# Rotary embedding over split heads: eight tiles of 8 rows a partition in place of a mix of 4 and 8, with the rows dealt anew to VectorE and TensorE

## The chip, the core and the metric

The kernel runs on one core of one Trainium2 chip. A core has five engines that run side by side: TensorE (PE, with its weight loads shown as PEld), VectorE (DVE), ScalarE (ACT), GpSimd (POOL) and SyncE (SP). Data moves between the device's memory (HBM) and the on-chip SBUF over 16 DMA engines. A DMA is issued from a queue; here ScalarE issues the loads and SyncE the stores. PSUM is the small memory that TensorE writes and that VectorE and ScalarE read. The metric is the device time of one execution in microseconds (us), as a median over runs; a change of under 0.5% is taken as no change.

## The reference

```
x = x.reshape(16, 512, 16, 64)                 # batch, seq, heads, head_dim
x1, x2 = x[..., :32], x[..., 32:]
cos = cos[None, :, None, :]                    # seq x 32
sin = sin[None, :, None, :]
rotated = concatenate([x1 * cos - x2 * sin, x1 * sin + x2 * cos], axis=-1)
```

x has 16 x 512 rows of 1024 float32 (4 KB), 33.55 MB in all, and the result has the same size. Each element of the result is the sum of two products: the element times a cosine, and its partner in the other half of the head times a sine with a sign. cos and sin depend on the place in the sequence alone and are 64 KB each.

## The kernel before

A "row" below is one row of x in each of 128 partitions, 128 x 1024 elements (512 KB). There are 64 of them, numbered u = 0 to 63. A batch of 512 rows gives each partition 4 consecutive rows (R1 = 4, a "single", 16 KB a partition); a pair of batches gives each partition 8 (R2 = 8, 32 KB a partition). Batches 0, 1, 14 and 15 are singles, the other twelve are six pairs, so there are ten tiles of 4, 4, 8, 8, 8, 8, 8, 8, 4 and 4 rows. They live in a ring of 40 rows in SBUF (x_sb) and are worked on in place.

Each row takes three steps. First, t1 = x times cosine, on VectorE, from SBUF into one of three PSUM slots (line 293). Second, t2 = x with its halves swapped, times the signed sine, into one of six SBUF slots; GpSimd does this (line 257) except for row 3 of each pair, which VectorE does (line 286, the list V2). Third, the sum t1 + t2 goes back over x. For most rows VectorE adds (line 304, called comb below). For the rows of the list PE2 (rows 1, 3 and 6 of each eight, outside the first and last four rows, 21 in all) TensorE adds t2 to t1 in PSUM by multiplying with the identity (line 224) and ScalarE copies PSUM to SBUF (line 191).

VectorE's order is written out by hand: for u = 0, 1, 2 ... it issues the cosine product of row u (with the sine product ahead of it, if row u is in V2) and then the sum of row u - 1, if that is VectorE's. The cosine product of row u must wait until the PSUM slot of row u - 3 is free, which for a row of PE2 is ScalarE's copy.

The sine and cosine tables are needed in two layouts. For singles VectorE copies the cosine (line 264) and ScalarE the sine (lines 182 and 183) straight from the staged tables. For pairs TensorE picks the staged rows into PSUM (line 208) and ScalarE copies the sine out with both signs (lines 186 and 187).

ScalarE issues six loads (40 rows) and the two tables at the start (lines 153 and 174). The other loads go over places of the ring whose rows must first be stored. ScalarE issues them in the midst of its copies, after the row with LAG = 10 added to the last row that held the place, that is after u = 17, 25 and 33, and waits there for the store of that place (line 146). SyncE issues one store a tile (line 161), when the tile's last row is added.

```
    singles = (0, 1, batch - 2, batch - 1)
    tiles = [(b, R1 if b in singles else R2) for b in range(batch) if b in singles or b % 2 == 0]
    V_ROW = 3
    PE2 = [R1 <= u < NU - R1 and u % R2 in (1, 3, 6) for u in range(NU)]
    V2 = [tiles[t][1] == R2 and r == V_ROW for t, r in rows]
```

Of the kernel before, what the change touches and what calls it, by code (L numbers as in the profile page):

```python
# [6 lines left out]
def bass_split_heads_rope_kernel(  # L7
# [9 lines left out]

    batch, seq, dim = x.shape
# [5 lines left out]
    R2 = 2 * R1  # L30
    assert R1 * P == seq and R1 == 4 and batch % 2 == 0
# [8 lines left out]
    singles = (0, 1, batch - 2, batch - 1)  # L40
    tiles = [(b, R1 if b in singles else R2) for b in range(batch) if b in singles or b % 2 == 0]
    NT = len(tiles)
    RING = 5 * R2

    rows = [(t, r) for t, (_, n) in enumerate(tiles) for r in range(n)]
    NU = len(rows)
    EARLY = (NU - RING) // R2


    V_ROW = 3  # L50
    PE2 = [R1 <= u < NU - R1 and u % R2 in (1, 3, 6) for u in range(NU)]
    V2 = [tiles[t][1] == R2 and r == V_ROW for t, r in rows]

# [12 lines left out]
    LAG = 10  # L66

    with ExitStack() as stack:
# [3 lines left out]
        s1_sb = stack.enter_context(nc.sbuf_tensor([P, R1, 2, HALF], fp32))  # L72
        s2_sb = stack.enter_context(nc.sbuf_tensor([P, R2, 2, HALF], fp32))
        ident = stack.enter_context(nc.sbuf_tensor([P, P], fp32))
        pick = stack.enter_context(nc.sbuf_tensor([P, 2, 2, P // 2], fp32))
        zero = stack.enter_context(nc.sbuf_tensor([P, BANK], bf16))
        tab_ps = stack.enter_context(nc.psum_tensor([P, BANK], fp32))
        pair_ps = stack.enter_context(nc.psum_tensor([P, 2, 2, R1, HALF], fp32))
        t1_ps = stack.enter_context(nc.psum_tensor([P, NT1, H * HD], fp32))
        sem_in = [stack.enter_context(nc.semaphore(f"in{t}")) for t in range(NT)]  # L80
        sem_out = [stack.enter_context(nc.semaphore(f"out{k}")) for k in range(EARLY)]
# [3 lines left out]
        sem_c = stack.enter_context(nc.semaphore("ctab"))  # L85
        sem_s = stack.enter_context(nc.semaphore("stab"))
        sem_z = stack.enter_context(nc.semaphore("zero"))
# [7 lines left out]
        sem_t = stack.enter_context(nc.semaphore("pairs"))  # L95
        sem_a = stack.enter_context(nc.semaphore("act"))

        c1_ps = tab_ps[:, 0:R1 * HALF].rearrange("p (r d) -> p r d", d=HALF)
        v_ps = tab_ps[:, R1 * HALF:R1 * HALF + HD].rearrange("p (t d) -> p t d", d=HALF)

        def c_of(t, r):
            return c1_ps[:, r, :] if tiles[t][1] == R1 else pair_ps[:, r // R1, 0, r % R1, :]

        def s_of(t, r):
            return s1_sb[:, r] if tiles[t][1] == R1 else s2_sb[:, r]

        x1 = x.rearrange("b (s r) d -> b s (r d)", r=R1)
        o1 = out.rearrange("b (s r) h d -> b s (r h d)", r=R1)
        x2 = x.rearrange("b s d -> (b s) d").rearrange("(g p r) d -> g p (r d)", p=P, r=R2)
        o2 = out.rearrange("b s h d -> (b s) h d").rearrange("(g p r) h d -> g p (r h d)", p=P, r=R2)  # L110
        xs = x_sb[:].rearrange("p n h t d -> p n (h t d)")

        def in_dram(single, pairs, t):
            b, n = tiles[t]
            return single[b] if n == R1 else pairs[b // 2]

        def in_sbuf(t):
            b, n = tiles[t]
            k = b * R1 % RING
            return x_sb[:, k:k + n].rearrange("p n h t d -> p (n h t d)")  # L120

        def where(u):
            t, r = rows[u]
            return t, r, u % RING

# [6 lines left out]
        def wait_added(eng, u):  # L132

            if n_pe[u]:
                eng.wait_ge(sem_a, n_pe[u])
            if n_comb[u]:
                eng.wait_ge(sem_v, n_comb[u])

        def wait_t2_free(eng, u):

# [7 lines left out]
        def stores_of(k):  # L148

            return sum(b * R1 // R2 == k for b, _ in tiles)  # L150

        def load(eng, t):
            eng.dma_start(in_sbuf(t), in_dram(x1, x2, t)).then_inc(sem_in[t], 16)  # L153

        def on_sync(sp):
            for u in range(NU):
                t, r, k = where(u)
                if r == tiles[t][1] - 1:
                    wait_added(sp, u)
                    k = u // R2  # L160
                    sp.dma_start(in_dram(o1, o2, t), in_sbuf(t)).then_inc(sem_out[k] if k < EARLY else sem_rest, 16)
            sp.wait_ge(sem_rest, 16 * sum(stores_of(k) for k in range(EARLY, NU // R2)))

        def on_scalar(ae):
            later = {}
            for t, (b, n) in enumerate(tiles):
                if b * R1 + n <= RING:
                    load(ae, t)
                else:

                    later.setdefault((b * R1 - RING) // R2 * R2 + R2 - 1 + LAG, []).append(t)
                if t == 0:
                    for i, (table, sem) in enumerate(((cos, sem_cos), (sin, sem_sin))):
                        ae.dma_start(stage[:, i, :], table.rearrange("(s r) d -> s (r d)", r=R1)).then_inc(sem, 16)  # L174

            ae.wait_ge(sem_i, 2)
            ae.activation(  # L177
                pick[:], ident[:].rearrange("q (s k) -> q k s", k=2)[:, :, None, :].broadcast_to([P, 2, 2, P // 2]), COPY
            ).then_inc(sem_g, 1)
# [54 lines left out]
        def on_gpsimd(pl):  # L234
# [11 lines left out]
            for u in range(NU):  # L246
                if V2[u]:
                    continue
                t, r, k = where(u)
                if (t, r) == (0, 0):  # L250
                    pl.wait_ge(sem_s, 1)
# [103 lines left out]
```

## Time and profile before

| what | value |
|---|---|
| median of 3 runs (161.09 to 161.94) | 161.11 us |
| the profiled execution's own time (its span, first to last instruction) | 160.0 us |
| median less that span | 1.1 us |
| bytes moved in the span, mean rate | 67.26 MB, 420 GB/s |
| busy: VectorE, GpSimd, TensorE, ScalarE | 130.1, 134.9, 73.7, 24.4 us |
| mean granted TensorE clock | 0.710 of full speed |
| DMAs on ScalarE's queue / SyncE's queue | 12 (33.69 MB) / 10 (33.56 MB) |

The page gives busy time for each engine as a share of the span, and the DMA line gives the mean share of the core's 16 DMA engines that were busy in each of 40 slices. The profile gives no time of that execution other than the span. Lines such as "ACT x_sb L191 <- PE t_ps L224: 98.9" say that ScalarE, at line 191, sat idle for 98.9 us in all until TensorE's line 224 was done. A DMA's "us to landing" runs from its issue to the arrival of its last byte, so it includes the time that it stands in its queue.

### The profile page before, as it was taken

To read this page: it belongs to the slowest core of one execution; us is meant where nothing else is said; L and a number is where in the kernel's file an instruction comes from. 1 tells how busy PE (TensorE), PEld (TensorE's weight loads), DVE (VectorE), ACT (ScalarE), POOL (GpSimd) and SP (SyncE) were. 2 spreads that over 40 slices of the span, in tenths; PEclk is the share of its full clock that TensorE was granted. 3 is DMA by queue.
4 is the path that set the end of the run, shared out by engine and by line. 5 is a ranking of instruction groups with operands and counts; after the bars stand their busy time and mean duration, and the time that the engine had idled before them with its cause. 6 is when DMAs were issued, how large, how long until landed. Compare 5 with 4: busy or idle time off the path is not lost.

```text
span 160.0 us, 522 instructions
## 1 busy us (share of the span) xinstructions
PE 73.7 (46%) x94; PEld 23.7 (15%) x94; DVE 130.1 (81%) x117; ACT 24.4 (15%) x27; POOL 134.9 (84%) x64
## 2 busy tenths in 40 slices
PE   6050005476427735690948606459439841970000
PEld 1020002021102220220222002002202210320000
DVE  0069998699999998997989709899999989989600
ACT  0420000205020502022022020220220122050000
POOL 1059999999999999999999999698999999289400
PEclk9999999969955865567555685855855599577555
DMA  5999999999999999999999999999999999999997
GB/s 160 401 451 463 401 430 418 410 483 406 401 463 406 494 401 401 483 426 401 467 426 418 410 467 434 401 467 393 420 463 446 418 414 418 479 410 434 414 414 303
DMA packets 3170, 67.26 MB, mean 420 GB/s; under 512 B 352, under 2 KB 608, under 8 KB 608
## 3 DMA queue, kind: packets, MB, share of 16 engines
q10 hardware_dynamic: 1728, 33.69, 49.7%
q1 hardware_dynamic: 1440, 33.56, 48.8%
q14 instruction: 2, 0.02, 0.0%
HBM read 33.69 MB, written 33.55 MB: 420 GB/s over the span
## 4 chain that ended last, share of the span: by engine, by line
DMA 59%; POOL 22%; PE 5%; DVE 3%; issue 2%; ACTq 1%; ACT 1%; DVEq 0%
DMA x_sb<-in_x_dram 41%; POOL t_sb L257 22%; DMA out_dram<-x_sb 18%; PE t_ps L224 5%; DVE x_sb L304 2%; DVE t_ps L293 1%; ACT x_sb L191 1%; ACTq L153 1%; ACTq L174 1%; DVEq L303 0%
## 5 line engine op out<-in xcount | busy, mean ns | idle before, releaser
L257 POOL TENSOR_TENSOR t_sb<-x_sb,s_sb 128x1024 f32<-128x1024 f32 x58 | 134.2, 2358 | 14.2 <-ACT s_sb L183 8.2
L224 PE MATMUL t_ps<-t_sb,ident 128*128 128x512 f32 x84 | 68.9, 973 | 62.8 <-DVE t_ps L293 37.9
L293 DVE TENSOR_TENSOR t_ps<-x_sb,pair_ps 128x1024 f32<-128x1024 f32 x48 | 57.7, 1223 | 9.7 <-ACT x_sb L191 9.7
L304 DVE TENSOR_TENSOR x_sb<-t_ps,t_sb 128x1024 f32<-128x1024 f32 x43 | 52.4, 1218 | 2.1 <-POOL t_sb L257 2.1
L191 ACT ACTIVATE x_sb<-t_ps 128x1024 f32<-128x1024 f32 x21 | 21.5, 1024 | 110.6 <-PE t_ps L224 98.9
L224 PEld LDWEIGHTS t_ps<-t_sb,ident 128*128 128x128 f32 x84 | 21.8, 286 | 109.6 <-DVE t_ps L293 70.0
L293 DVE TENSOR_TENSOR t_ps<-x_sb,tab_ps 128x1024 f32<-128x1024 f32 x16 | 19.3, 1222 | 0.5 <-ACT x_sb L191 0.5
L286 DVE TENSOR_TENSOR t_sb<-x_sb,tab_ps 128x1024 f32<-128x1024 f32 x6 | 7.3, 1212 | 0.0
L264 DVE COPY tab_ps<-stage 128x128 f32<-128x128 f32 x1 | 0.3, 295 | 7.7 <-DMA stage<-in_cos_dram 7.7
L208 PE MATMUL pair_ps<-stage,pick 128*128 128x256 f32 x4 | 2.0, 667 | 5.1 <-DMA stage<-in_sin_dram 5.1
L201 PE MATMUL t_ps<-zero 128*128 128x512 bf16 x6 | 2.7, 630 | 1.3 <-DVE zero L262 1.3
L208 PEld LDWEIGHTS pair_ps<-stage,pick 128*128 128x128 f32 x4 | 1.2, 324 | 6.2 <-issue 6.0
L177 ACT ACT_TABLE_LOAD x1 | 1.3, 1283 | 5.0 <-issue 5.0
L201 PEld LDWEIGHTS t_ps<-zero 128*128 128x128 bf16 x6 | 0.7, 138 | 2.3 <-DVE zero L262 1.2
L262 DVE MEMSET zero<- 128x256 uint32 x1 | 0.3, 272 | 0.9 <-PEq L337 0.9
L182 ACT ACTIVATE s_sb<-stage 128x128 f32<-128x128 f32 x1 | 0.3, 310 | 2.3 <-DMA stage<-in_sin_dram 2.3
L186 ACT ACTIVATE s_sb<-pair_ps 128x256 f32<-128x256 f32 x1 | 0.4, 384 | 1.7 <-PE pair_ps L208 1.7
L235 POOL MEMSET ident<- 128x128 f32 x1 | 0.2, 205 | 0.3 <-POOLq L337 0.3
L177 ACT ACTIVATE pick<-ident 128x256 f32<-128x256 f32 x1 | 0.4, 430 | 0.0
L187 ACT ACTIVATE s_sb<-pair_ps 128x256 f32<-128x256 f32 x1 | 0.4, 377 | 0.0
L237 POOL TENSOR_SCALAR_AFFINE_SELECT ident<-ident 128x128 f32<-128x128 f32 x1 | 0.3, 294 | 0.1
L337 POOL MEMSET const-float32-0.0<- 128x1 f32 x1 | 0.1, 99 | 0.3 <-issue 0.3
(6 smaller groups left out, 1.0 us busy)
## 6 DMA issues: line engine op xcount, KB each, us to landing
x_sb<-in_x_dram ACTq DMA_DIRECT2D x6, 4096.0 KB, 38.1
out_dram<-x_sb SPq DMA_DIRECT2D x6, 4096.0 KB, 25.3
x_sb<-in_x_dram ACTq DMA_DIRECT2D x4, 2048.0 KB, 22.4
out_dram<-x_sb SPq DMA_DIRECT2D x4, 2048.0 KB, 14.9
stage<-in_cos_dram ACTq DMA_DIRECT2D x1, 64.0 KB, 7.6
stage<-in_sin_dram ACTq DMA_DIRECT2D x1, 64.0 KB, 7.3
```

The lines of the kernel that those rows point to most:

```text
L153: eng.dma_start(in_sbuf(t), in_dram(x1, x2, t)).then_inc(sem_in[t], 16)
L174: ae.dma_start(stage[:, i, :], table.rearrange("(s r) d -> s (r d)", r=R1)).then_inc(sem, 16)
L177: ae.activation(pick[:], ident[:].rearrange("q (s k) -> q k s", k=2)[:, :, None, :].broadcast_to([P, 2, 2, P // 2]), COPY).then_inc(sem_g, 1)
L186: ae.activation(s2[:, :, :, 0, :], pair_ps[:, :, 1, :, :], COPY, scale=-1.0)
L191: ae.activation(xs[:, u % RING, :], t1_ps[:, u % NT1, :], COPY).then_inc(sem_a, 1)
L201: pe.matmul(t1_ps[:, k, b * BANK:(b + 1) * BANK], zero[:, 0:P], zero[:], start=True, stop=True).then_inc(sem_w, 1)
L208: pe.matmul(pair_ps[:, k].rearrange("p c r d -> p (c r d)"), pick[:, k].rearrange("q b s -> q (b s)"), stage[:].rearrange("q c f -> q (c f)"),
L224: ins = pe.matmul(t1_ps[:, u % NT1, b * BANK:(b + 1) * BANK], ident[:], t2[:, b * BANK:(b + 1) * BANK], start=False, stop=True, skip_group ...
L257: pl.tensor_tensor(t2_sb[:, u % NT2, :, :, :], swapped(k), over_heads(s_of(t, r)), mult).then_inc(sem_p, 1)
L286: ve.tensor_tensor(t2_sb[:, u % NT2, :, :, :], swapped(k), over_heads(v_ps), mult)
L293: ve.tensor_tensor(t1_ps[:, u % NT1, :].rearrange("p (h d) -> p h d", d=HALF), x_sb[:, k, :, :, :].rearrange("p h t d -> p (h t) d"), c_of ...
L304: ve.tensor_tensor(xs[:, k, :], t1_ps[:, u % NT1, :], t2_sb[:, u % NT2, :, :, :].rearrange("p h t d -> p (h t d)"), add,).then_inc(sem_v, 1)
```

## The change

Every tile has 8 rows (32 KB a partition), so one layout of the tables is left. Tile k takes rows 8k to 8k + 7, still in a ring of 40 rows. Only the load of tile 0 and the store of tile 7 are cut into two DMAs of 4 rows. There are 9 loads, 9 stores and the 2 tables: 20 DMAs in place of 22. The early loads (rows 0 to 39) have the same order and the same sizes as before. The late loads (tiles 5, 6 and 7) are issued behind rows 17, 25 and 33, as before, and wait for the stores of tiles 0, 1 and 2; the last is now one DMA of 8 rows, not two of 4.

The rows are dealt anew. PE2 is every odd row from 3 to 59 (29 rows, 21 before). V2 is rows 3 and 6 of each tile (16 rows, 6 before). GpSimd keeps 48 rows (58 before), and VectorE adds 35 rows (43 before). The rows of the first tile, whose first four took their tables straight from the staged ones, now wait for TensorE's picking too: TensorE picks cosine and sine in four matmuls of 128 columns (two of 256 before), the sine through one of the t1 slots. VectorE makes its own signed sines (two small instructions) ahead of row 2.

```diff
-    singles = (0, 1, batch - 2, batch - 1)
-    tiles = [(b, R1 if b in singles else R2) for b in range(batch) if b in singles or b % 2 == 0]
-    NT = len(tiles)
-    RING = 5 * R2
...
-    V_ROW = 3
-    PE2 = [R1 <= u < NU - R1 and u % R2 in (1, 3, 6) for u in range(NU)]
-    V2 = [tiles[t][1] == R2 and r == V_ROW for t, r in rows]
+    TILES = (
+        (8, 0, (4, 4), (8,), ()),
+        (8, 8, (8,), (8,), ()),
+        (8, 16, (8,), (8,), ()),
+        (8, 24, (8,), (8,), ()),
+        (8, 32, (8,), (8,), ()),
+        (8, 0, (8,), (8,), (0,)),
+        (8, 8, (8,), (8,), (1,)),
+        (8, 16, (8,), (4, 4), (2,)),
+    )
+    RING = 40
+
+    BEHIND = {6: 17, 7: 25, 8: 33}
...
+    V_ROWS = {8: (3, 6)}
+    V2 = [r in V_ROWS[TILES[t][0]] for t, r in rows]
+
+    PE2 = [2 <= u < NU - R1 and u % 2 == 1 for u in range(NU)]
...
         def on_scalar(ae):
...
+            early = [i for i in range(len(loads)) if i not in late]
+            for i in early:
+                load(ae, i)
...
-            ae.wait_ge(sem_sin, 16)
-            sv = stage[:, 1, :].rearrange("s (r d) -> s r d", d=HALF)
-            ae.activation(s1_sb[:, :, 0, :], sv, COPY, scale=-1.0)
-            ae.activation(s1_sb[:, :, 1, :], sv, COPY).then_inc(sem_s, 1)
...
+            for i, n in enumerate(SIZES):
+                ae.wait_ge(sem_t, i + 1)
+                ae.activation(s_sb[n][:, :, 0, :], raw_sin[n], COPY, scale=-1.0)
+                ae.activation(s_sb[n][:, :, 1, :], raw_sin[n], COPY).then_inc(sem_s, 1)
             for u in range(NU):
                 if PE2[u]:
                     ae.wait_ge(sem_e, n_pe[u])
...
+                for i in late:
+                    if BEHIND[i] == u:
+                        for j in TILES[loads[i][0]][4]:
+                            ae.wait_ge(sem_out[j], 16)
+                        load(ae, i)
...
+            for n in SIZES:
+                for c, to in enumerate((c_ps[n], raw_sin[n])):
+                    for k in range(n // R1):
+                        ins = pe.matmul(
+                            to[:, k * R1:(k + 1) * R1, :].rearrange("p r d -> p (r d)"),
+                            pick[n][:, k].rearrange("q b s -> q (b s)"),
+                            stage[:, c, :],
+                            start=c == 0,
+                            stop=True,
+                            skip_group_check=c == 1,
+                        )
+                ins.then_inc(sem_t, 1)
...
+            def own_sines():
+                ve.wait_ge(sem_s, len(SIZES))
+                for n in SIZES:
+                    v = V_ROWS[n]
+                    some = raw_sin[n][:, v[0]:v[-1] + 1:max(1, v[-1] - v[0]), :]
+                    ve.tensor_scalar_mul(v_ps[n][:, :, 0, :], some, -1.0).then_inc(sem_k, 1)
+                    ve.tensor_copy(v_ps[n][:, :, 1, :], some).then_inc(sem_k, 1)
+                ve.wait_ge(sem_k, 2 * len(SIZES))
...
+                if u == NT1 - 1:
+                    own_sines()
```

## The prediction

> **What bounds the kernel now.** I read the page first, its slices and its DMA queues, then three long windows, then the DMA issues one by one, and last the waits and the stretch around the longest one. The page's slices show how full the DMA engines are:
>
> ```profile
> DMA  5999999999999999999999999999999999999997
> GB/s 160 401 451 463 401 430 418 410 483 406 401 463 406 494 401 401 483 426 401 467 426 418 410 467 434 401 467 393 420 463 446 418 414 418 479 410 434 414 414 303
> q10 hardware_dynamic: 1728, 33.69, 49.7%
> q1 hardware_dynamic: 1440, 33.56, 48.8%
> ```
>
> The two queues' packets fill 98.5% of 16 engines' span: only 2.4 of 160.0 us are not DMA. The view by windows (columns: time, busy PE, PEld, DVE, ACT, POOL, then clock, DMA share, GB/s) splits this into loads alone, both queues, and stores alone:
>
> ```profile
> 2.50:20.00 17.50, 3.54 (x8) 1.48 (x6) 10.58 (x10) 2.88 (x6) 10.38 (x5) 1.00 0.98 416
> 24.00:138.00 114.00, 64.00 (x78) 20.26 (x79) 103.34 (x93) 19.46 (x19) 110.51 (x48) 0.67 1.00 431
> 140.50:158.00 17.50, 2.44 (x4) 0.67 (x2) 9.42 (x9) 1.59 (x2) 9.24 (x4) 0.60 0.98 422
> ```
>
> Whichever queue has work, the engines are full and the rate stays near 430 GB/s. So the DMA engines bound the kernel, one queue is enough to fill them, and the compute engines matter only where they leave both queues empty. The end shows how near that is, in the timeline (start, duration) and the DMA issues in the window of the last store:
>
> ```profile
> 149.84 1.23 DVE L304 TENSOR_TENSOR x_sb<-t_ps,t_sb 128x1024 f32<-128x1024 f32 x1 [0.67 <-POOL t_sb L257]
> 151.14 0.33 SPq L161 DMA_DIRECT2D out_dram<-x_sb  x1
> ...
> out_dram<-x_sb SPq DMA_DIRECT2D x1, 2048.0 KB, 8.8
> ```
>
> The last store is issued at 151.1 and lands at 160.0. In the packet records a 16 KB packet takes 0.611 us and a 32 KB one 1.213; the store has 8 of 16 KB on each engine, 4.9 us. So it stood about 3.6 us behind the store before it: compute has a few us to spare. Around the longest wait ScalarE and VectorE show this:
>
> ```profile
> ACT x_sb L191 <- DMA out_dram<-x_sb: 3.6, 1, 3.6
> 92.80 2.31 ACTq L153 DMA_DIRECT2D x_sb<-in_x_dram  x2
> 95.16 1.02 ACT L191 ACTIVATE x_sb<-t_ps 128x1024 f32<-128x1024 f32 x1 [8.17 <-issue]
> 96.21 1.23 DVE L293 TENSOR_TENSOR t_ps<-x_sb,pair_ps 128x1024 f32<-128x1024 f32 x1 [5.09 <-ACT x_sb L191]
> 97.50 3.78 PE L224 MATMUL t_ps<-t_sb,ident 128*128 128x512 f32 x4 [7.05 <-DVE t_ps L293]
> ```
>
> ScalarE waits for a store before it may issue a late load; its next copy is late, and VectorE loses 5.1 us. This wait stays in the change.
>
> **The change, part by part.** *DMA bill.* 256 pairs of 16 KB packets become single 32 KB ones: 256 x (2 x 0.611 - 1.213) = 2.3 us over 16 engines, 0.15 us less. Two DMAs fewer: nothing, since no window shows a gap at their joints. The early loads are the same. A DMA bound gives 160.0 - 0.15 = 159.85 us, if a queue is always filled. The rest is that question.
>
> *Tables.* They start when the staged tables are in, at 9.1. Before, four passes of 256 columns took 2.05 us; now eight of 128, each with its weight load (0.32). Least: the same 2.05. Most: nothing overlaps, 8 x (0.32 + 0.26) = 4.6. I take 2.9, eight weight loads with the passes under them, because line 224's loads (0.34) do lie under its passes. ScalarE's two copies took 0.7 (11.23 to 11.89). GpSimd starts at 12.8, not 9.6. Covered by 20 MB of loads already queued (49 us).
>
> *Tile 0.* GpSimd's pitch is 2.315 (20.82 / 9), so row 0's sine product ends at 15.15 and VectorE's first sum at 16.3. Its small sine instructions (0.19 each and a wait, 0.4 in all) and eleven more operations at its back-to-back pitch of 1.133 (120.87 to 125.40 in four) end row 7's product at 29.2. TensorE adds 3.78 at half clock (1.98 at full, as at 36.62) and ScalarE 1.02: the first store goes at 34.1, or 32.3 at full clock; before it was 20.25. That costs nothing while loads fill the engines.
>
> *Balance.* GpSimd goes from 58 to 48 rows, 111 us. VectorE goes from 64 + 6 + 43 = 113 to 64 + 16 + 35 = 115 operations, 130 us, and is now the slowest. A tile is 14 of them, 15.9 us. TensorE's four rows at half clock take 15.1 us, so they fit. From the end of a cosine product to ScalarE's release is 3.78 + 1.02 + 0.13 = 4.93 us against four VectorE operations between (4.5); that wait comes once a tile (behind V2 rows there are five operations) at 0.49, as a release at 102.37 shows. A tile is 16.35 us. GpSimd needs 13.9 and runs ahead in the six slots.
>
> *Stores and loads.* With both queues on 32 KB packets each gets half: 19.4 us per 4 MB, as in the stores that landed at 73.2 and 92.8 (issue plus time to landing). The first store before had its first packet 3.6 us after issue, behind loads. So stores 0, 1, 2 land at 34.1 + 3.6 + 19.4 + 0.6 = 57.7, then 77.2 and 96.7. Loads run alone until 37.7 (9.7 us a tile), then at half rate: tiles 3 to 7 land at 48, 68, 87, 107 and 126. Before, the last load came at 140.4. From 126 the store queue has three tiles left: it is the one to be kept full.
>
> *ScalarE's waits.* Tile 2 starts on VectorE at 46.7; behind row 17 (copied at 54.4) the wait until 57.7 holds up nothing, since ScalarE's next copy is due at 57.9. Behind row 25 (70.7) the wait lasts until 77.2 and VectorE loses 2.6 us. Behind row 33 it waits for store 2, at 96.7: with issue (0.33) and copy (1.02) VectorE goes on at 98.2 from row 38 and has lost 3 us more. Compute after that hangs on store 2. SyncE and TensorE wait behind it in their own order only; GpSimd has filled its slots.
>
> *The tail.* From 98.2 VectorE has 3 + 14 + 14 + 16 = 47 operations (the last tile has two more sums, having no TensorE rows after 59): 53.3 us, three waits of 0.49, and the last sum's end: 153.0. At full clock store 2 is 1.8 earlier and the waits go: 149.8. Needed: the bound's end 159.85 less 0.35 (last packet to end) less 4.9 puts the last store's first packet at 154.6; a queue that isn't shared starts 1.0 after issue (first load: 0.81 to 1.83), so the issue is due by 153.6. It makes it, by 0.6 at half clock and 3.8 at full. Tile 6's last copy (138.2, due by 139.1) and the first half of tile 7 (146.6, due by 148.8) also do. So the sum is 159.85, and with the 1.1 by which the median stands over this profile's span, 161.0: no change.
>
> [...]
>
> **The rivals.** *The last store comes too late (slower).* The mechanism is ScalarE's wait for store 2, from which all of the last 47 VectorE operations hang. It decides from 153.6, one us for each. For it: the slack is 0.6 at half clock; tables at 4.6 cost 1.7 of it; an issue like the second half of the 2.31 above (1.94, not 0.33) costs 1.6; a queue latency of 3.6 costs 2.6. Against: before, full clock came back in stretch after stretch, and a store behind another is already in the queue while that runs. Two of these at half clock, say the tables and the issue, put it at 156.3, so 2.7 late: 163.7. One: 162.1. As its time I take 162.8.
>
> *The last load is late as before (slower).* If it landed at 140.4 as before, a whole tile would follow: 16 x 1.133 + 0.5 = 18.6, then 1.0 + 4.9 + 0.35: 165.3, median 166.4. Against: the late half tiles then had 16 KB packets against 32 KB stores, a third of the rate; now halves meet.
>
> *DMAs cost something apiece (faster).* The packet records hold 1.4 us of longer packets, 0.86 at the start and 0.54 mostly near 22 to 27 where the first store joined. If the joining falls away and the rows' ends are more even over the engines (first engine lands at 158.9, last at 160.0), the gain is some 1.1: 160.0. Against: the start is unchanged and the joining only moves.
> [...]
>
> **How the numbers follow.** 0.5% of 161.1 is 0.8 us, about what a measurement of this kernel tells from no change. No change 0.67, at 161.0; the late last store 0.23; the late load 0.03; faster 0.07. The last three lie beyond 0.8 us. The range goes from 160.2 (most of the faster case) to 163.3 (most of the late store, up to about two of its costs).
>
> **What would show it.** Right: DMA share still about 98% with both queues together; first store near 32 to 34; last load landing near 126; VectorE waiting for ScalarE near 75 and 95; last store issued between 150 and 153.6; its time to landing over 6. Wrong: a DMA gap in the last slices and a last store that lands within some 6 us of issue; loads landing after 130; windows with both queues above 435 GB/s.

## The result

The change made the kernel a little slower. Its median is 162.11 us (161.9 to 162.78, six runs) against 161.38 us (161.09 to 161.94, six runs) for the kernel before on the same chip: a ratio of 1.0053, with an interval of 1.0034 to 1.0072. (Ratios and their 95% intervals, here and below, compare the fast runs alone and are not the quotients of the medians beside them.) A second set on another chip gave 161.86 against 161.34, 1.0028 [1.0009, 1.0047]. So the loss is 0.3 to 0.5%, where 161.0 and "no change" were forecast; the time lies inside the forecast range of 160.2 to 163.3. Against the 0.5% set ahead as the line for no change, the first set lies just above it and the second under it; both intervals leave out 1, so the loss is small but real. The profiled execution has a span of 161.1 us and took 162.40.

The page of the kernel after, its slices of the DMA engines and its DMA queues (columns of the queues: packets, MB, share of 16 engines):

```profile
DMA  5999999999999999999999999999999999999994
GB/s 171 412 427 456 456 456 391 456 358 488 391 399 513 391 401 496 391 415 496 391 407 505 391 399 496 407 399 480 411 407 464 433 399 464 431 407 427 415 439 175
q10 hardware_dynamic: 1584, 33.69, 49.4%
q1 hardware_dynamic: 1296, 33.56, 48.3%
q8 instruction: 1, 0.02, 0.0%
q14 instruction: 2, 0.02, 0.0%
```

Three things are to be seen. The slices are full from end to end, as before. The last slice holds 175 GB/s where the page of before had 303: most engines have run out of work while the span goes on. And there is a row that the page of before does not have, q8, a queue of kind "instruction" with one packet. In the packet records this is 16,384 bytes, 0.935 us long, at 115.05 us. The page of before has one row of this kind, which stands there below the two that the forecast showed, with two packets of 8,192 bytes, 0.309 us each:

```profile
q14 instruction: 2, 0.02, 0.0%
```

The same three windows as before the change (time, busy PE, PEld, DVE, ACT, POOL, then clock, DMA share, GB/s):

```profile
2.50:20.00 17.50, 3.54 (x12) 2.08 (x10) 8.08 (x9) 2.37 (x4) 8.19 (x4) 1.00 0.99 421
24.00:138.00 114.00, 69.06 (x108) 23.58 (x108) 107.14 (x95) 27.41 (x27) 92.57 (x41) 0.82 1.00 429
140.50:158.00 17.50, 0.24 (x1) 0.00 (x0) 9.89 (x9) 1.02 (x1) 4.20 (x2) 0.64 0.98 420
```

The engines were as full as before in each (0.99, 1.00 and 0.98 against 0.98, 1.00 and 0.98), so no queue ran dry. What differs comes after 158 us. The same view for the last two microseconds, first the kernel before and then the kernel after:

```profile
159.00:160.00 1.00, 0.00 (x0) 0.00 (x0) 0.00 (x0) 0.00 (x0) 0.00 (x0) 0.50 0.04 16
160.00:161.00 1.00, 0.00 (x0) 0.00 (x0) 0.00 (x0) 0.00 (x0) 0.00 (x0) 0.50 0.00 0
```

```profile
159.00:160.00 1.00, 0.00 (x0) 0.00 (x0) 0.00 (x0) 0.00 (x0) 0.00 (x0) 0.50 0.12 49
160.00:161.00 1.00, 0.00 (x0) 0.00 (x0) 0.00 (x0) 0.00 (x0) 0.00 (x0) 0.50 0.04 16
```

A share of 0.04 with 16 GB/s is one packet of 16 KB in that microsecond, counted where it starts. Before, one such packet started after 159.0 and none after 160.0; after, three and one. The events with which each of the 16 engines reports its part of the last store say the same: before, the first engine lands at 158.91, the median at 159.44 and the last at 159.96; after, at 158.71, 159.02 and 161.02. Most engines are done earlier than before, three later than the last of before (160.30, 160.47 and 161.02), and the span ends with the last of them, 1.06 us later.

The last store is not late from compute (timeline, and the DMA issues in the window of that store, with KB and us to landing):

```profile
148.04 2.35 DVE L338 TENSOR_TENSOR x_sb<-t_ps,t_sb 128x1024 f32<-128x1024 f32 x2
150.46 0.33 SPq L190 DMA_DIRECT2D out_dram<-x_sb  x1
...
out_dram<-x_sb SPq DMA_DIRECT2D x1, 2048.0 KB, 10.6
```

It is issued at 150.46, 0.7 us earlier than before, and lands 10.6 us later; it stands in its queue behind the store before it.

The wait of ScalarE that the forecast followed, in the list of waits and then in the timeline around the third of them:

```profile
ACT x_sb L215 <- DMA out_dram<-x_sb: 22.2, 3, 8.9
DVE t_ps L328 <- ACT x_sb L215: 7.2, 7, 2.9
```

```profile
94.37 0.33 ACTq L177 DMA_DIRECT2D x_sb<-in_x_dram  x1
94.75 1.94 ACT L215 ACTIVATE x_sb<-t_ps 128x1024 f32<-128x1024 f32 x2 [8.61 <-DMA out_dram<-x_sb]
95.81 2.36 DVE L328 TENSOR_TENSOR t_ps<-x_sb,tab_ps 128x1024 f32<-128x1024 f32 x2 [2.92 <-ACT x_sb L215]
```

ScalarE sits 22.2 us in three waits for stores, 18.6 more than the page of before puts down to stores. It costs VectorE 2.9 us here, as forecast, and the end nothing.

### The profile page after: what moved, and what is told of

Its sections match the earlier page's. It is cut to its first block, busy times and chain, and to the rows that moved or that the text cites. A ratio compares the mean times of both kernels' runs of the same rounds, so it can differ in the third digit from the quotient of the medians.

```text
span 161.1 us, 585 instructions
## 1 busy us (share of the span) xinstructions
PE 80.1 (50%) x130; PEld 28.1 (17%) x130; DVE 131.6 (82%) x118; ACT 31.8 (20%) x33; POOL 112.2 (70%) x54
## 4 chain that ended last, share of the span: by engine, by line
DMA 45%; DVE 25%; issue 10%; PE 6%; POOL 4%; ACT 2%; ACTq 1%; DVEq 0%; POOLq 0%
DMA x_sb<-in_x_dram 23%; DMA out_dram<-x_sb 18%; DVE t_ps L328 13%; DVE x_sb L338 10%; PE t_ps L253 4%; POOL t_sb L286 4%; DMA stage<-in_sin_dram 4%; DVE t_sb L316 3%; ACT x_sb L215 1%; PE tab_ps L236 1%; PE t_ps L236 1%; ACTq L199 0%; ACT sine L210 0%; ACTq L177 0%; ACT sine L211 0%
## 5 line engine op out<-in xcount | busy, mean ns | idle before, releaser
L286 POOL TENSOR_TENSOR t_sb<-x_sb,sine 128x1024 f32<-128x1024 f32 x48 | 111.5, 2358 | 31.9 <-DMA x_sb<-in_x_dram 16.2
L253 PE MATMUL t_ps<-t_sb,ident 128*128 128x512 f32 x116 | 75.3, 798 | 54.4 <-DVE t_ps L328 52.5
L328 DVE TENSOR_TENSOR t_ps<-x_sb,tab_ps 128x1024 f32<-128x1024 f32 x64 | 76.1, 1223 | 17.1 <-PE t_ps L236 9.9
L215 ACT ACTIVATE x_sb<-t_ps 128x1024 f32<-128x1024 f32 x29 | 29.5, 1023 | 100.7 <-PE t_ps L253 78.5
L253 PEld LDWEIGHTS t_ps<-t_sb,ident 128*128 128x128 f32 x116 | 25.6, 244 | 103.6 <-DVE t_ps L328 79.7
L338 DVE TENSOR_TENSOR x_sb<-t_ps,t_sb 128x1024 f32<-128x1024 f32 x35 | 42.5, 1216 | 0.8 <-POOL t_sb L286 0.8
L316 DVE TENSOR_TENSOR t_sb<-x_sb,tab_ps 128x1024 f32<-128x1024 f32 x16 | 19.4, 1210 | 0.0
L236 PE MATMUL tab_ps<-stage,chosen 128*128 128x128 f32 x4 | 1.2, 454 | 4.9 <-DMA stage<-in_sin_dram 4.9
L236 PE MATMUL t_ps<-stage,chosen 128*128 128x128 f32 x4 | 1.1, 421 | 0.0
L236 PEld LDWEIGHTS t_ps<-stage,chosen 128*128 128x128 f32 x4 | 1.0, 333 | 0.0
```

The lines of the kernel that those rows point to most:

```text
L215: ae.activation(xs[:, place_of(u), :], t1_ps[:, u % NT1, :], COPY).then_inc(sem_a, 1)
L236: ins = pe.matmul(to[:, k * R1:(k + 1) * R1, :].rearrange("p r d -> p (r d)"), pick[n][:, k].rearrange("q b s -> q (b s)"), stage[:, c, :] ...
L253: ins = pe.matmul(t1_ps[:, u % NT1, b * BANK:(b + 1) * BANK], ident[:], t2[:, b * BANK:(b + 1) * BANK], start=False, stop=True, skip_group ...
L286: pl.tensor_tensor(t2_sb[:, u % NT2, :, :, :], swapped(place_of(u)), over_heads(s_sb[n][:, r]), mult).then_inc(sem_p, 1)
L316: ve.tensor_tensor(t2_sb[:, u % NT2, :, :, :], swapped(k), over_heads(v_ps[n][:, V_ROWS[n].index(r)]), mult,)
L328: ve.tensor_tensor(t1_ps[:, u % NT1, :].rearrange("p (h d) -> p h d", d=HALF), x_sb[:, k, :, :, :].rearrange("p h t d -> p (h t) d"), c_ps ...
```

## The experiments

The theory from the two profiles: the rows given to TensorE lengthen its instruction stream, the stream then needs one more fetch of 16 KB, that fetch runs on one of the 16 DMA engines, and since all of them are full to the end, the engine that had it ends last and so sets the time. Rivals: the new tiles cost it, by the way loads and stores meet on the engines; the later compute costs it; or nothing but chance in which engine ends last.

Here is what the traces show of the last store on the 16 engines (first, median and last to land, us) and of the fetch. Records of packets carry no engine number; an engine is followed by joining packets whose end meets the next one's start. "Delay" is what the packet behind the fetch on its engine took beyond its usual time.

| kernel | first | median | last | 16 KB fetch at | it took + delay |
|---|---|---|---|---|---|
| before | 158.91 | 159.44 | 159.96 | none | |
| before, again | 158.86 | 159.36 | 160.05 | none | |
| after | 158.71 | 159.02 | 161.02 | 115.1 | 0.935 + 0.494 |
| after, again | 158.87 | 159.04 | 160.47 | 114.9 | 0.935 + 0.494 |
| tiles alone | 158.71 | 159.05 | 160.04 | none | |
| deal alone | 158.99 | 159.24 | 160.67 | 118.3 | 0.939 + 0.491 |
| stream alone | 158.96 | 159.59 | 160.41 | 137.3 | 0.879 + 0.547 |
| tiles alone, later loads (b3) | 158.99 | 159.15 | 160.48 | none | |
| after, later loads (c4) | 158.90 | 159.25 | 160.53 | 108.0 | 0.881 + 0.401 |
| before, later loads (d4) | 158.93 | 159.49 | 160.17 | none | |

These are single executions, and they differ by some tenths of a microsecond from one to the next; the medians carry the argument. The profile of b3, with no fetch and a last landing at 160.48, was the slowest of that kernel's twelve (162.07, median 161.58). That of the stream alone was among its fastest (161.69, from 161.59 to 162.91).

**The first set: the halves of the change, and the stream by itself.** The kernel after was run again, unchanged (a1_again).

> The changed kernel once more, for a second profile and a tighter interval. In its first profile the last store is issued at 150.5 us, in time, yet the 16 DMA engines finish unevenly: the first at 158.7, the last at 161.0 (before: 158.9 and 160.0). If that is a property of the kernel (both theories), the ratio is again 1.003 to 1.007, the span 160.6 to 161.4, and the spread of the last store's 16 landings again about 2 us or more. If it was chance, the spread is near 1 us in this profile and the ratio near 1.000.

Measured: 161.86 against 161.34, 1.0028 [1.0009, 1.0047]. The fetch is there at the same place and the last engine lands at 160.47. It is not the engine that had the fetch: that one's last packet ends at 159.98, the last engine's at 160.15, after 1.7 us of longer packets. (A landing is reported 0.3 to 0.4 us after the engine's last packet.)

Next, the new tiles and tables with the rows dealt as before (a2_tiles_old_deal):

```diff
-    V_ROWS = {8: (3, 6)}
+    V_ROWS = {8: (3,)}
-    PE2 = [2 <= u < NU - R1 and u % 2 == 1 for u in range(NU)]
+    PE2 = [R1 <= u < NU - R1 and u % 8 in (1, 3, 6) for u in range(NU)]
```

> The eight tiles with the rows dealt as before (TensorE rows 1, 3 and 6 of eight, VectorE sine row 3): TensorE's stream is then about as short as before. Theory B (instruction fetch): the changed kernel has a third instruction fetch, 16 KB on a queue of its own at 115 us, which TensorE's longer stream calls for and which costs one DMA engine 0.94 us and 0.49 more on the packet behind it; without it the ratio is 0.998 to 1.002 and that queue is missing. Theory A (tiles): one DMA engine loses 0.2 to 0.7 us at each landing of a 4 MB store while loads run; this stays with the tiles, so ratio 1.003 to 1.007 and a landing spread of 2 us.

Measured: 161.66 against 161.34, 1.0005 [0.9978, 1.0032]. Its queues:

```profile
q10 hardware_dynamic: 1584, 33.69, 49.7%
q1 hardware_dynamic: 1296, 33.56, 48.6%
q14 instruction: 2, 0.02, 0.0%
```

It has the packets of the kernel after and no q8. The tiles alone cost between nothing and 0.3%.

The other half is the tiles of before with the new deal (a3_old_tiles_new_deal):

```diff
-    V_ROW = 3
-    PE2 = [R1 <= u < NU - R1 and u % R2 in (1, 3, 6) for u in range(NU)]
-    V2 = [tiles[t][1] == R2 and r == V_ROW for t, r in rows]
+    V_ROWS = (3, 6)
+    PE2 = [2 <= u < NU - R1 and u % 2 == 1 for u in range(NU)]
+    V2 = [tiles[t][1] == R2 and r in V_ROWS for t, r in rows]
```

> The tiles of before with 29 rows for TensorE (odd rows 3 to 59) and VectorE's own sines in rows 3 and 6 of each pair. Theory B: the 16 KB instruction fetch appears and the ratio is 1.002 to 1.007. Theory A: the tiles are those of before, so ratio 0.998 to 1.002 and a landing spread near 1 us, whether or not the fetch appears.

Measured: 162.05 against 161.34, 1.0038 [1.0018, 1.0057]. The instruction queues of its page:

```profile
q8 instruction: 1, 0.02, 0.0%
q14 instruction: 2, 0.02, 0.0%
```

The fetch is back and so is the loss. Here the engine that had the fetch is the one that ends last: its last packet ends at 160.30, the next engine's at 159.73.

The deal changes more than the length of a stream, so the fourth kernel is the kernel before, whole, with 40 tiny products of zeros ahead of the tables, in time in which TensorE only waits for the staged tables (a4_before_long_stream):

```diff
+            for _ in range(40):
+                pe.matmul(pair_ps[0:32, 0, 0, 0, :], zero[:, 0:32], zero[:, 0:HALF], start=True, stop=True)
             pe.wait_ge(sem_g, 1)
```

> The kernel before with 40 tiny matmuls more on TensorE (with their weight loads 80 instructions) while it waits for the tables: nothing else is changed and no other work is in their way. Theory B: the 16 KB instruction fetch appears, and the ratio is 1.001 to 1.006 according to which DMA engine it falls on. Theory A: ratio 0.999 to 1.001, with or without the fetch.

Measured: 161.96 against 161.34, 1.0043 [1.0018, 1.0069]. TensorE's timeline at the start, and the instruction queues:

```profile
3.92 1.19 PE L205 MATMUL pair_ps<-zero 128*32 128x32 bf16 x40
9.08 2.05 PE L210 MATMUL pair_ps<-stage,pick 128*128 128x256 f32 x4 [3.96 <-DMA stage<-in_sin_dram]
```

```profile
q8 instruction: 1, 0.02, 0.0%
q14 instruction: 2, 0.02, 0.0%
```

The 40 products took 1.19 us and were done 3.96 us before the staged tables came, so no later work was held up by them; the tables start at 9.08, before at 9.1. The granted clock between 2.5 and 20 us is 0.65 where it was 1.00, but the tables take 2.05 us all the same. What they leave is the 16 KB fetch, 132 us later, at 137.3. The last packet on its engine ends last (159.99, the next engine's at 159.53), and the loss is that of the whole change. Of the rivals, the tiles are not present in this kernel. Compute is a little later in this execution, with the last store issued at 151.81 against 151.14, but that did not hold up the end: joined up, the packets leave no gap of over 0.02 us on any engine from 3 us to its last packet.

**The second set: more and less of it.** If the length of the stream decides, four rows fewer on TensorE might do without the fetch (b1_short_stream, on the kernel after):

```diff
-    V2 = [r in V_ROWS[TILES[t][0]] for t, r in rows]
-    PE2 = [2 <= u < NU - R1 and u % 2 == 1 for u in range(NU)]
+    V2 = [r in V_ROWS[TILES[t][0]] and not (t < 4 and r == 6) for t, r in rows]
+    PE2 = [2 <= u < NU - R1 and u % 2 == 1 and not (u < 32 and u % 8 == 7) for u in range(NU)]
```

> The changed kernel, but four of TensorE's rows (row 7 of tiles 0 to 3) go back to VectorE and four of VectorE's sines (row 6 of the same tiles) to GpSimd, so that TensorE has 25 rows, between the 21 and the 29 of the runs so far, and VectorE has as many operations as in the changed kernel. Theory B (the 16 KB instruction fetch of TensorE's long stream is the loss): if the fetch is missing the ratio is 0.998 to 1.002, if it is there 1.003 to 1.005. Against it, a theory that the denser use of TensorE and ScalarE itself delays the DMA engines: some 1.002 to 1.003 either way.

Measured: 162.78 against 161.27, 1.0098 [1.0074, 1.0123]: slower, not faster. The fetch was still there, at 140.1, so the run says nothing of a shorter stream without it. By the recorded TensorE instructions, kernels with 206 (before) and 214 (tiles alone) have no fetch, and those with 249 (this one), 278, 285 and 286 have one; 526, in the next kernel, has two. A loss twice as large is not explained by the fetch. In this profile, in order of landing, all 16 engines end 0.3 to 1.1 us later than in the kernel after, not one alone.

Then 160 tiny products in place of 40, on the kernel before (b2_before_longer_stream; only the 40 of the diff above becomes 160).

> The kernel before with 160 tiny matmuls in TensorE's wait for the tables (40 in a4; they took 1.2 us there, so 4.8 us here, still ahead of the tables). Theory B: TensorE's stream is longer by 320 instructions, so more 16 KB fetches than the one of a4 appear, each 0.9 us on one DMA engine and some 0.5 on the packet behind it. If they fall on the same engine, the ratio is 1.009 to 1.013, if on different ones 1.004 to 1.007. If the number of fetches has nothing to do with the stream: as in a4, 1.004, with one fetch.

Measured: 162.39 against 161.27, 1.0055 [1.0034, 1.0076].

```profile
q8 instruction: 2, 0.03, 0.1%
q14 instruction: 2, 0.02, 0.0%
```

Two fetches, at 9.9 and 114.5. The last packet on the second's engine ends last (160.77, the next engine's at 159.93). The loss is like that with one fetch, within the intervals, as was expected if the two fell on different engines.

The next kernel tests the rival of loads and stores that meet. In the records of after, some load packets near 53 to 118 us are longer than usual, most of them right after a store on the same engine was completed, 0.19 us to an engine on average (0.03 of it is the packet behind the fetch). The kernel with the tiles alone was given later loads, so that no load is issued at the moment of a store's landing (b3_late_loads):

```diff
-    BEHIND = {6: 17, 7: 25, 8: 33}
+    BEHIND = {6: 22, 7: 30, 8: 41}
```

> As a2 (eight tiles, old deal), but the three late loads are issued behind rows 22, 30 and 41, not 17, 25 and 33, some us after the store that they wait for has landed. In the profiles, the DMA engine that lands last has packets longer by 0.1 to 0.6 us around the landings at 55, 75 and 94. Theory C: the load that is issued at that moment disturbs the engine that is still busy; then the long packets go, the last engine ends 0.3 to 0.8 us earlier and the ratio is 0.995 to 0.999. If the landing itself (the store's completion on that engine) makes the next read long, nothing changes against a2: 0.999 to 1.002. The loads have time in either case: the queue holds 16 us of earlier loads at each point.

Measured: 161.58 against 161.27, 1.0021 [1.0011, 1.0032]. The longer packets are gone (0.00 us; 0.03 with the old places) and nothing is won. The interval, beside that of the same tiles with the old places of the loads (1.0005 [0.9978, 1.0032]), leaves room for a cost of the tiles of 0.1 to 0.3% without any 16 KB fetch.

The fourth kernel asks whether a fetch of another engine's instructions does the same: 60 memsets of one column each on VectorE, at the start, in the kernel before (b4_before_long_vector):

```diff
+        scrap = stack.enter_context(nc.sbuf_tensor([P, 60], fp32))
...
             ve.memset(zero[:], 0.0)
+            for i in range(60):
+                ve.memset(scrap[:, i:i + 1], 0.0)
```

> The kernel before with 60 tiny fills on VectorE in its wait for the tables. The two 8 KB instruction fetches of before come when VectorE (or GpSimd) has run some 64 instructions. Theory B in its general form: VectorE's longer stream moves its fetch forward in time or adds another of 8 KB: 0.31 us and 0.1 to 0.36 on the packet behind it, on one engine. That is less than the last engine's lead over most others, so ratio 0.999 to 1.003, and the fetch that came at 55.7 us comes earlier. If those fetches are GpSimd's alone, their number and times stay as they are.

Measured: 166.88 against 161.27, 1.0264 [1.0213, 1.0316], far more than the fetch of TensorE's. VectorE's timeline and the instruction queue:

```profile
1.15 1.48 DVE L265 MEMSET scrap<- 128x1 f32 x60
9.92 2.36 DVE L296 TENSOR_TENSOR t_ps<-x_sb,tab_ps 128x1024 f32<-128x1024 f32 x2
```

```profile
q14 instruction: 3, 0.02, 0.0%
```

The memsets end 7.3 us before VectorE's first product, so they hold up none of its work. They move a packet of 8 KB to 6.7 us, where the loads start, and add a third. In the records of before the two packets come when VectorE has started 64 and 128 of its recorded instructions (55.73 and 114.67 us), in those of after 63 and 138 (58.17 and 128.31). The profiled execution took 164.16, less than its median by 2.7, so it holds only part of the loss: 0.87 us of longer load packets to an engine, and a last engine that lands at 162.71, 3.3 after the first. A packet of 0.309 us, with 0.53 on the packet behind it, does not account for that.

**The third set: the loads' places.** The short stream was run again (c1_short_stream_again, the kernel of b1 unchanged).

> The kernel of b1 once more, as the control of c2 on the same chip. In b1 every DMA engine ended 0.7 to 1.0 us later than in the changed kernel, and reads in the stretch from 50 to 130 us were 0.68 us longer in sum on each engine (0.08 to 0.19 in the changed kernel). If that is a property of the kernel, ratio 1.007 to 1.012 again and the sum 0.5 us or more; if it was that chip or chance, 1.003 to 1.005 and the sum under 0.2.

Measured: 162.54 against 161.30, 1.0102 [1.0063, 1.0141]. The 1.0% stands, on another chip. In this profile the longer load packets are 0.16 us to an engine, where b1 had 0.67, so they do not explain it.

Later loads for it (c2_short_stream_late_loads), and for the kernel after (c4_after_late_loads), with the same edit:

```diff
-    BEHIND = {6: 17, 7: 25, 8: 33}
+    BEHIND = {6: 23, 7: 31, 8: 41}
```

> b1 with the late loads behind rows 23, 31 and 41 instead of 17, 25 and 33, so that none is issued at the moment when the store it waits for lands. Theory C (the load issued at the landing lengthens the reads of all engines then): the sum of longer reads falls from 0.68 to under 0.1 us an engine and the ratio from 1.0098 to 1.002 to 1.005. If the long reads have another cause: as c1.

> The changed kernel with the late loads behind rows 23, 31 and 41. VectorE no longer waits for ScalarE's waits near 76 and 96, so the last store is issued some 2 us earlier, near 148; that is worth nothing if the DMA engines are the bound. The 16 KB instruction fetch stays. Theory B alone: ratio 1.002 to 1.005 as before. If the loads issued at the landings cost the last engine its time (0.2 to 0.6 us in the two profiles), 1.000 to 1.002.

Measured: c2 162.14 against 161.30, 1.0057 [1.0036, 1.0078], which overlaps the interval of c1, so a gain is unclear; c4 161.95 against 161.30, 1.0036 [1.0023, 1.0048], the loss of the kernel after. The longer packets are at 0.00 us in both, and the fetch stays (137.1 and 108.0). With them gone, the engine with the fetch is the last in both profiles: its last packet ends at 160.24 in c2 and 160.13 in c4, the next engine's at 159.44 and 159.48. Taking the longer packets away does not win back what the change lost. Nor do the waits of ScalarE matter to the end, since c4 has none for stores and loses the same.

Later loads for the kernel with the 60 memsets (c3_long_vector_late_loads; LAG = 16 in place of 10):

> b4 (60 tiny fills on VectorE, 1.0264) with LAG = 16 instead of 10, so that the late loads are issued some us after the stores have landed. Theory C: the longer reads (0.87 us an engine between 50 and 130) go and the ratio falls to 1.005 to 1.015; what is left is the early fetch on one engine and its lag. If the lag alone makes the loss, the ratio stays at 1.02 to 1.03.

Measured: 168.19 against 161.30, 1.0418 [1.0357, 1.0479]. So the places of the loads are not what cost b4 its 2.6%. Whether the longer packets are is not settled, since here the later loads did not remove them (0.60 us to an engine, 0.87 in b4). The run shows what the forecast's two late rivals look like. Its timeline at the end, and the DMA issues in the window of the last store:

```profile
146.08 9.26 POOL L258 TENSOR_TENSOR t_sb<-x_sb,s_sb 128x1024 f32<-128x1024 f32 x4 [6.34 <-DMA x_sb<-in_x_dram]
155.45 1.23 DVE L307 TENSOR_TENSOR x_sb<-t_ps,t_sb 128x1024 f32<-128x1024 f32 x1 [1.08 <-POOL t_sb L258]
```

```profile
out_dram<-x_sb SPq DMA_DIRECT2D x1, 2048.0 KB, 8.7
```

GpSimd waits 6.34 us for the last load, which comes at 146.0; its four rows take 9.26 us, VectorE's last sum ends at 156.7, the last store is issued at 156.75 and lands at 165.4. In the kernel before, the last load is in at 140.4 and the store issued at 151.14; in the kernel after, at 130.7 and 150.46. The load is late on three engines only: 13 of the 16 have their part of it in by 139.3 (median 139.0, before 139.8), and the other three at 144.3, 144.4 and 146.0. From load to load the last engine falls behind the median: by 0.8 us at 14.3, 1.9 at 72.5, 5.8 at 130.3 and 7.0 at 146.0. b4 shows the same, smaller (three engines at 140.5 to 142.1, median 139.1). Why these engines fall behind is open.

**The fourth set: one engine's extra time by itself.** The kernel before was run against itself (d1_before_again).

> The kernel before once more, for a second profile of it and as a control of the ratio itself: 0.999 to 1.001. If the spread of the last store's landings (1.0 us from the first to the last DMA engine) belongs to the kernel, it is 0.8 to 1.3 us again, and no 16 KB instruction fetch is there.

Measured: 161.36 against 161.29, 1.0003 [0.9992, 1.0013]. Differences of 0.3% are beyond this.

Then the kernel before with a small load that runs on one DMA engine only: 17 partitions of 2 KB, which go as 17 packets of 0.084 us, one after the other, 1.43 us in all, as much as the fetch's 0.94 and its delay together. That the number 17 is what keeps it on one engine is not shown. SyncE issues it late, near 118.6 (d2_extra_load_late):

```diff
+        scrap = stack.enter_context(nc.sbuf_tensor([17, 512], fp32))
...
+                if u == 47:
+                    sp.dma_start(scrap[:], x.rearrange("b s d -> (b s) d")[0:17, 0:512]).then_inc(sem_x, 16)
```

> The kernel before with one more DMA of 34 KB into unused SBUF, 17 partitions of 2 KB, which falls on a single DMA engine (17 does not divide over 16), some 1.3 us of its time by the 16 KB packets' 0.611; SyncE issues it near 119 us ahead of a store. No instruction stream grows by more than a few. Theory B (the slowest of 16 full engines sets the time, and a fetch is one engine's extra work): that engine ends 1.3 us later than it would, 159.9 to 160.9, so ratio 1.001 to 1.006. If the loss of the long streams has another cause than the engine's time: 0.999 to 1.001.

Measured: 162.47 against 161.29, 1.0066 [1.0044, 1.0088]. The DMA issues near it (KB; the records give no landing for it):

```profile
out_dram<-x_sb SPq DMA_DIRECT2D x1, 4096.0 KB, 21.9
scrap<-in_x_dram SPq DMA_DIRECT2D x1, 34.0 KB
```

34 KB against the 67,000 of the kernel. Spread over 16 engines its 1.43 us would be 0.09 us, 0.06% of the time, far under the interval's 0.44%. On one engine it costs 0.7 to 1.4 us by the interval, about what was expected (up to 1.006), and that engine is the last to end (its last packet at 159.95 in the profiled execution, which at 161.73 was the fastest of ten).

The same load, issued by ScalarE right behind the tables, where it runs at 8.3 to 9.8 us (d3_extra_load_start):

> The same extra load, but issued by ScalarE right behind the tables, so that the one engine is 1.3 us behind from the start. If a lag only adds: 1.001 to 1.006, as d2. If an engine that lags from the start loses more and more against the others, which would explain the 1.026 and 1.042 of b4 and c3 with their fetch at 7 us: 1.01 to 1.04.

Measured: 161.93 against 161.29, 1.0037 [1.0023, 1.0051]. An engine is again alone at the end, its last packet at 160.26 and the next engine's at 159.56. The lag is still there 150 us later: the last engine is behind the median by 1.6 us in the load that lands at 15.3, by 2.7 in the last load (142.40) and by 1.2 at the end (160.60), where the kernel before has 0.5, 0.6 and 0.5. So a lag of 1.43 us is not made up where the engines are full. It does not grow to anything like the 7.0 us of c3 either, and by itself it does not explain b4 and c3.

Last, the kernel before with later loads (d4_before_late_loads, LAG = 16):

> The kernel before with LAG = 16, the late loads some us after the landings: in c2, c4 and b3 this took the longer reads between 50 and 130 us from 0.03 to 0.16 us an engine to 0.00. In the profile of before the last engine has some 0.7 us of them. If they go and nothing comes in their place, ratio 0.996 to 0.999, the best so far; if the last engine lags anyway, 0.999 to 1.002.

Measured: 161.44 against 161.29, 1.0004 [0.9990, 1.0018]. This kernel had next to nothing to win there: its longer load packets are 0.03 us to an engine, in the two profiles of before 0.08 and 0.02. No version beat the kernel before; the two nearest to it are this one and the tiles alone.

**What is shown, and what stays open.** Shown: a longer stream on TensorE, in time in which it had nothing to do, brings the 16 KB fetch and a loss of 0.4%; 1.4 us on one of 16 full engines costs 0.7 to 1.4 us; the deal alone has fetch and loss, the tiles alone no fetch and 0 to 0.3%. Over all sets, kernels without the 16 KB fetch, and without memsets or an extra load, stand at 1.0003 to 1.0021 (a2, b3, d1, d4) and those with it at 1.0028 to 1.0057 (the kernel after, a1, a3, a4, b2, c2, c4) or at 1.010 (b1, c1).

That the fetch costs its time on one engine is the step between, and it is argued from the sizes (1.43 us against d2's 1.43) and from the engine that ends last. That engine is the fetch's in a3, a4, b2, c2 and c4, but not in a1, b1 and the first profile of the kernel after. In the last, the fetch's engine had its last packet end at 160.09 and would have been near 158.7 without 1.43 us; the engine that ended last, at 160.69, had no fetch but 2.2 us of longer packets, 1.0 of it right behind completed stores. So that one execution would have ended where it did without the fetch, and without the longer packets still some 0.5 us later than before. In c2 and c4 the longer loads are gone, the fetch's engine alone is left behind, and the loss is still there.

Open are the growing lag of three engines in b4 and c3 (2.6 and 4.2%, without a 16 KB fetch), why b1 and c1 lose 1.0%, and which instruction calls for the fetch.

## Why the prediction was right or wrong

- *DMA bill: wrong, and this is the step that failed.* Its own size was right: the first engine lands 0.20 us earlier than before, against the 0.15 worked out, and the median engine 0.4 earlier. But the bill counted loads and stores only and took 16 engines as one. There was no term for a fetch of instructions (1.43 us with its delay, on one engine), and none for the last engine, with which the span ends. It lands 1.06 us later in the profiled execution, and the median rose by 0.5 to 0.7 us where 0.15 less was billed. That the time still fell within the range is luck: the range reached up for a last store that comes too late, which did not happen. The condition that it named, a queue that is always filled, was met.
- *Tables: bounds right, value too high.* Eight passes took 2.06 us, the lower bound of 2.05, not the 2.9 taken. The timeline:

```profile
8.91 1.19 PE L236 MATMUL tab_ps<-stage,chosen 128*128 128x128 f32 x4 [4.92 <-DMA stage<-in_sin_dram]
9.90 1.06 PE L236 MATMUL t_ps<-stage,chosen 128*128 128x128 f32 x4
11.81 6.95 POOL L286 TENSOR_TENSOR t_sb<-x_sb,sine 128x1024 f32<-128x1024 f32 x3 [10.44 <-ACT sine L211]
```

  The two groups overlap: the weight loads lie under the passes here too. GpSimd starts at 11.81, not 12.8.
- *Tile 0: right with full clock.* The first store goes at 31.45; 32.3 was worked out for full clock and 34.1 for half, and the 1.0 us of GpSimd's earlier start makes up the difference.
- *Balance: right.* GpSimd is busy for 112.2 us (111 forecast) and VectorE for 131.6 (130), the slowest.
- *Stores and loads: right in kind, the stores 2 to 3 us early, the loads 3 to 5 us late.* Stores 0, 1 and 2 land at 54.95, 75.0 and 94.35, against 57.7, 77.2 and 96.7, early by what tile 0 was. The loads of tiles 3 to 7 are all in at 51.4, 71.5, 91.2, 110.9 and 130.7 (on the first engine 1.6 to 3.5 us sooner), against 48, 68, 87, 107 and 126. So the last load came after 130, which the forecast had named as a sign of being wrong; the last store was still issued in time.
- *ScalarE's waits: right.* VectorE's longest wait for ScalarE is 2.9 us, against 2.6 and 3.
- *Tail: right.* The last store is issued at 150.46, within 149.8 to 153.0 and 3.1 before it was due, and lands over 6 us later.
- *Clock: nearer to full than before.* The tail was worked out for half clock (153.0) and for full (149.8). The mean granted clock went from 0.710 to 0.824, with 69.06 us of matmul in the long window against 64.00; that the one follows from the other is not shown.
- *The rivals.* The late store and the late load did not come. c3, made from the kernel before, shows both; that its span of 165.4 is near the 165.3 of the late load is chance, since there the load comes at 146.0 with four rows to follow, where the rival had 140.4 and eight. The rival with fewer DMAs was half right: most engines did end earlier, but not more evenly (2.3 us from first to last, 1.05 before), and the last engine sets the end. Missing was a rival in which the sign turned on one engine of 16. The page of before had a row that pointed to it, "q14 instruction", two packets of instructions among the data; the forecast makes no use of it.

In the traces TensorE's fetch is one packet of 16,384 bytes on a queue apart from the data (q8). The packets on q14 are of 8,192 bytes, and b4 shows that some of them are VectorE's: 60 memsets more bring one from 55.7 to 6.7 us and add a third. A longer stream on TensorE is not free in this kernel, whose DMA engines are full (share 1.00 from 24 to 138 us): a4 measured 1.0043 [1.0018, 1.0069] for the stream alone.

## What to carry to other kernels

Where all the DMA engines are full to the end, as here, the end is set by the slowest of 16, not by their mean (in the kernel after 161.02 us, with the median engine at 159.02): read the landing of the last DMA engine by engine, and count everything that runs on a single engine, whenever it runs (1.43 us on one engine measured 1.0037 at 8.3 us in d3 and 1.0066 near 118.6 in d2). The instructions are part of that traffic (16,384 bytes on q8 here), so rows moved to a compute engine with time to spare can still cost, if they make its stream longer (a3, 1.0038); compare the "instruction" rows of the two queue lists first. A few tenths of a percent of this kind are told from noise only by a run of the kernel against itself beside it (d1, 1.0003 [0.9992, 1.0013]).

## What was not expected of the hardware

- One fetch of 16 KB took 0.88 to 1.01 us, where a data packet of the same size takes 0.611, and the packet behind it on its engine 0.39 to 0.55 us more than usual.
- 1.43 us of extra work on one DMA engine at 8 to 10 us was not made up: the last engine was 1.6 us behind the median just after it and 1.2 at 160.6 us, where the kernel before has 0.5 at both (d3).
- 60 memsets of one column, 1.48 us of VectorE in time in which it had nothing to do, cost 2.6% (b4). It brought a packet of instructions to 6.7 us, and three of the 16 DMA engines fell 1.4 to 3.0 us behind the median by the last load (5.3 to 7.0 us in c3). No run here explains why.
- Some load packets ran 0.1 to 0.6 us longer, most of them right behind a store's completion on the same engine. Issuing the loads a few rows later took them away in the kernels of eight tiles (0.00 us in b3, c2 and c4), not in c3 (0.60), and changed no median beyond its interval. The cause is not shown: of the eight that ran over 0.1 us longer in the kernel after, without the one behind the fetch, three were under way when a late load was issued (at 75.02 and 94.37), and two, at 113.0 and 113.8, had no load issued near them.
